# Three reorderings in a streaming encoder layer: where the sample sums and the keys' low part are split, which of two gate products comes first, and when the last hidden forms are made

## The chip, the cores and the metric

The kernel runs on one core of one Trainium2 chip. Its engines are named as in the profile: PE (matrix products), PEld (its weight loads), DVE (elementwise on vectors), ACT (activations, copies, casts), POOL (further elementwise work and a DMA queue), SP (a DMA queue). The metric is the time of one execution on the device in microseconds (us), median of the runs shown.

## The reference

One layer is computed for 512 prompt frames and 64 frames of a running stream, 576 in all, in fp32. Cut to what matters:

```python
hn = rmsnorm(x, g_norm1);  proj = hn @ w_in            # 2048 -> q, k, v (8 heads x 128), gb, gc, hc (1024 each)
z = q @ k.T / sqrt(128)                                # strictly causal
log_1mb = where(mask, log_sigmoid(-z), 0)
after = cumsum(log_1mb, axis=3, reverse=True) - log_1mb
w = where(mask, exp(log_sigmoid(z) + after), 0);  o_attn = w @ v
o_conv = gb * conv3_causal(gc * hc)
x = x + concat(rmsnorm(o_attn), rmsnorm(o_conv)) @ w_out
x = x + (silu(h2 @ w_gate) * (h2 @ w_up)) @ w_down     # h2 = rmsnorm(x, g_norm2), 2048 -> 5632 -> 2048
```

The running stream's 64 frames see 512 cached keys and values as well as their own.

## The kernel before

**Products in two parts.** Each fp32 operand is split into a high part (rounded to the product's format by an ACT cast) and a low part (DVE subtracts the high part from the source). A product of two operands is then three matmuls: high by high, low by high, high by low. `split(hi, lo, src)` issues the cast on ACT and the subtraction on DVE. Tiles that end in h and l (`qh`, `ql`, `kh`, `kl`, `sph`, `spl`, `ph1`, `pl1`) are such pairs; `whl` holds both parts of a weight block.

**Seven products instead of eight.** The large products run in units: two blocks of 128 output columns by two halves of 288 frames. A unit takes seven products, numbered `p_` = 1 to 7, of 24 matmuls each (fewer in the down projection). `run(n, p_)` issues product p_ of unit n; `prepare(n, p_)` splits the weight block that it needs, four places ahead in a list `order` (`AHEAD` = 4). Sums of weight blocks are made on DVE by `weight_sums` (lines L344 to L352). Products 1, 6, 5 and, later, 3 add up in one PSUM bank `psy`; after 1, 6 and 5 ACT copies what stands there (`part`, L427). Products 7 and 4 add up in a second bank, `psw`, and product 2 has a third, `psx`. After product 5 DVE adds a part and the bank to make results (L1491): for units 0 and 1 first half (0, 1) from bank `psv`, then half (1, 1) from `psw`. Units 0 and 1 of the feed-forward stage are "early": their product 3 has its own bank `psv`, taken from the three banks of the pool that `psy` comes from.

**What sets the order.** PE's instructions stand in the order in which the code issues them. The Python code advances generators by ticks: one tick is three matmuls of a large product, and a generator yields the number of ticks until its next step. In the attention and the gate/up stages a scheduler orders ACT, DVE, POOL and SP by its own estimate; `tc.issue_after(x)` holds work back behind instruction x. From the last gate/up units on, the order of these engines is the code's own (`manual_schedule`).

**Attention.** Eight heads pass through `attend(h)`, a new one every 29 ticks, between matmuls of the output projection (`pjo`). A head computes scores by key blocks 2, 1, 0 into banks z2, z1, z0, their softplus, sums over later keys by triangular products, and then, block by block, a mask (DVE, L1214), an exponential (ACT, L1216) and a split of the weights (`weights(b)`). For block 2 there are two masks, since block 3 shares its bank. The stream's own sums lie in `sp`, split into `sph` and `spl` and used by `sample_weights` (L1204 to L1207). The next head's queries and keys are split from `qf` and `kf` into `qh`, `ql`, `kh`, `kl`; PE first reads them for the next head's block 2 (L1161).

**Last hidden forms.** Gate and up columns come in 22 pairs. For each pair DVE makes seven combinations ("forms"), split and stored to `hid_dram`, which the down projection reads. Those of the last pair are made by `last_forms`, a generator that starts with a wait of 34 ticks and runs beside the first down products.

Of the kernel before, what the change touches and what calls it, by code (L numbers as in the profile page):

```python
# [10 lines left out]
F32 = mybir.dt.float32  # L11
F32R = mybir.dt.float32r
AF = mybir.ActivationFunctionType
ALU = mybir.AluOpType
PSUM = bass.MemoryType.PSUM

P = 128
TP = 512
# [6 lines left out]
NH = 8  # L25
# [76 lines left out]
def tile_hybrid_stream_step(  # L102
# [6 lines left out]
    nc = tc.nc  # L109
# [116 lines left out]
    def split(hi, lo, src, lo_eng=None):  # L226
        cast = nc.scalar.copy(out=hi, in_=src)  # L227
        (lo_eng or nc.vector).tensor_tensor(out=lo, in0=src, in1=hi.bitcast(F32), op=ALU.subtract)  # L228
        return cast.ins
# [731 lines left out]
    for E, h, lag in ((e1[0], 2, 8), (e1[1], 3, 22), (e0[0], 0, 36), (e0[1], 1, 50)):  # L961
# [4 lines left out]
    opening = [(0, 1), (0, 2), (1, 1), (0, 3), (0, 6), (1, 2), (0, 5), (0, 7), (1, 3), (0, 4), (1, 6), (2, 1), (1, 5),  # L966
               (1, 7), (2, 2), (1, 4), (2, 6), (2, 7), (2, 5)]
    order = [(n - NA, p_) for n, p_ in opening]
# [35 lines left out]
    qf, kf = (bpool.tile([P, T], F32, name=name) for name in ("qf", "kf"))  # L1004
    qh, ql, kh, kl = (bpool.tile([P, TP], F32R, name=name) for name in ("qh", "ql", "kh", "kl"))
# [4 lines left out]
    m01, mneg = (bpool.tile([P, P], F32, name=name) for name in ("m01", "mneg"))  # L1010
# [3 lines left out]
    sph, spl = (bpool.tile([P, T], F32R, name=name) for name in ("sph", "spl"))  # L1014
# [5 lines left out]
    def load_qk(h):  # L1020
        nc.sync.dma_start(out=qf, in_=qk_dram[h, 0])
        nc.sync.dma_start(out=kf, in_=qk_dram[h, 1])

    def split_qk():
        split(qh, ql, qf[:, :TP])
        split(kh, kl, kf[:, :TP])
# [7 lines left out]

    load_qk(0)
    split_qk()
    load_cached_keys(0)
    fetch_v(0)
# [111 lines left out]
    def attend(h):  # L1150
        pr, ph, pl, s1h, s1l, sp = (bt[n] for n in ("pr", "ph", "pl", "s1h", "s1l", "sp"))
        pb = [pr[0], pr[1], pr[2][:, :256], pr[2][:, 256:]]
        z, zb = {}, {}

        def scores(i):
            kk, q0 = slice(i * P, (i + 1) * P), i * P
# [39 lines left out]
        for b in (2, 1, 0):  # L1196
            nc.gpsimd.tensor_tensor(out=sums[:, b * TS : (b + 1) * TS], in0=sums[:, (b + 1) * TS : (b + 2) * TS],
                                    in1=sp[:, (b + 1) * TS : (b + 2) * TS], op=ALU.add)
# [12 lines left out]

        def weights(b):
            for i in ((2, 3) if b == 2 else (b,)):
                nc.vector.scalar_tensor_tensor(out=zb[i][:, :P], in0=zb[i][:, :P], scalar=0.0, in1=mneg,  # L1214
                                               op0=ALU.min, op1=ALU.add)
            nc.scalar.activation(out=pr[b][:, : full[b]], in_=z[b][:, : full[b]], func=AF.Exp)  # L1216
            return split(ph[b], pl[b], pr[b][:, : width[b]])

# [6 lines left out]
        mm(zb[2], trir, ph[2], stop=False, **kw)  # L1225
        mm(zb[2], trir, pl[2], stop=True, **kw)
        behind = weights(2)
        if h + 1 < NH:
            with tc.issue_after(behind):
                split_qk()  # L1230
        yield 4
        mm(zb[1], trir, ph[1], stop=False, **kw)
        mm(zb[1], trir, pl[1], stop=False, **kw)
        mm(zb[1][:, P:], neg1r, s1h, stop=False, **kw)
        mm(zb[1][:, P:], neg1r, s1l, stop=True, **kw)
        behind = weights(1)
        with tc.issue_after(behind):
            split(sph, spl, sp)
        yield 4
        mm(zb[0], trir, ph[0], stop=False, **kw)  # L1240
        mm(zb[0], trir, pl[0], stop=False, **kw)
        mm(zb[0][:, P:], neg1r, s0h, stop=False, **kw)
        mm(zb[0][:, P:], neg1r, s0l, stop=True, **kw)
        weights(0)
        hi, lo = mixa[h]
        ga, accA = col("ga", h), bt["accA"]
# [45 lines left out]
    def heads():  # L1292
        yield 9
        open_b()
        yield 3
        for h in range(NH):
            pipe.spawn(attend(h))
            yield PERIOD
# [135 lines left out]
    def put_form(fp, n, src):  # L1434

        t = tmp.tile([P, 2, HALF], F32R, tag="hl", name="form")
        split(t[:, 0], t[:, 1], src)
        q = nc.gpsimd if fp == NFP - 1 else nc.sync
        q.dma_start(out=hid_dram[fp][2 * n - 2 : 2 * n].rearrange("f p t -> p f t"), in_=t.bitcast(F32))  # L1439
# [26 lines left out]
    def last_forms(s10):  # L1466
        fp, h, tt = NFP - 1, hid.pop(NFP - 1), nc.vector.tensor_tensor
        s00, s01, s11 = h[0, 0], h[0, 1], h[1, 1]
        yield 34
        tt(out=s01, in0=s01, in1=gates.pop((0, 1)), op=ALU.mult)  # L1470
        yield 5
        tt(out=s10, in0=s10, in1=R2[:, :HALF], op=ALU.mult)
        tt(out=s10, in0=s10, in1=gates.pop((1, 0)), op=ALU.mult)
        for n, out, a, b in ((2, s10, None, None), (5, s00, s01, s00), (7, s01, s01, s11), (6, s11, s11, s00),
                             (4, s10, s10, s11)):
            yield 10
            if a is not None:
                tt(out=out, in0=a, in1=b, op=ALU.subtract)
            put_form(fp, n, out)

    def finish(kind, fp, c, i, ps, part=None):

        a, b = HALVES[i]
        if kind == "gate":
            s = gates[c, i] = tmp.tile([P, HALF], F32, tag="r" if i else "y", name="gs")
        else:
            s = tmp.tile([P, HALF], F32, tag="sq", name="ut") if c == i else h2pool.tile([P, HALF], F32, tag="hx", name="ux", bufs=2)
        if part is None:
            nc.vector.tensor_tensor(out=s, in0=ps, in1=R2[:, a:b], op=ALU.mult)
        else:  # L1490
            nc.vector.tensor_tensor(out=s, in0=ps, in1=part, op=ALU.add)  # L1491
            if kind == "up" and fp == NFP - 1 and (c, i) == (1, 0):
                pipe.spawn(last_forms(s))
                return
            nc.vector.tensor_tensor(out=s, in0=s, in1=R2[:, a:b], op=ALU.mult)
        if kind == "up" and fp == NFP - 1 and (c, i) == (0, 1):
            hid[fp][c, i] = s
            return
        if kind == "gate":
            nc.scalar.activation(out=s, in_=s, func=AF.Silu)  # L1500
            return
        nc.vector.tensor_tensor(out=s, in0=s, in1=gates.pop((c, i)), op=ALU.mult)
        hid.setdefault(fp, {})[c, i] = s
        put_forms(fp, c, i)

    slots = {}

    order = [(0, 1), (0, 2), (1, 1), (0, 3), (0, 6), (1, 2), (0, 7), (0, 5)] + opening[8:]
    early = {0, 1}
    for n in range(2, NU):  # L1510
        if n == NGU - 2:
# [183 lines left out]
```

## Time and profile before

| | us |
|---|---|
| median of 3 runs | 2346.3 (2346.07 to 2347.65) |
| profiled execution, its own time | 2347.48 |
| span of that execution, first to last instruction | 2345.8 |
| PE busy | 2332.0 (99% of the span) |
| DVE busy | 1940.0 (83%) |
| ACT busy | 1239.2 (53%) |
| POOL busy | 294.2 (13%) |

The mean granted clock of PE is 1.000. The attention stage lies between about 587 and 757 us of the span, the first gate and up products begin at 858.67 us, and the last forms fall between 1854 and 1880 us. Times in rows of the timeline are microseconds from the start of the span: start, duration, engine, line, operation, output<-inputs, shapes and count; in brackets stands how long the engine had been idle before the row and what ended the idle time.

### The profile page before, as it was taken

How to read it: one execution, taken by the hardware profiler on the slowest of the kernel's cores; microseconds unless marked ns; L12 is line 12 of the kernel's file. 1: busy time of each engine (PE TensorE's matmuls, PEld its weight loads, DVE VectorE, ACT ScalarE, POOL GpSimd, SP SyncE). 2: the span in 40 equal slices, each digit the busy share in tenths (PEclk: the TensorE clock that was granted, in tenths of full speed). 3: DMA queues.
4: the chain of work that ended last, by engine and by line, in shares of the span. 5: the costliest groups of instructions: out<-in, count | busy, mean ns of one | idle time of the engine just before them, and what ended most of it. 6: DMA issues, size and time to landing. Idle time of an engine off the chain costs nothing. (4 is left out here: it accounts for less than half of the span.)

```text
span 2345.8 us, 43802 instructions
## 1 busy us (share of the span) xinstructions
PE 2332.0 (99%) x17561; PEld 2321.6 (99%) x17561; DVE 1940.0 (83%) x2834; ACT 1239.2 (53%) x2244; POOL 294.2 (13%) x374
## 2 busy tenths in 40 slices
PE   9999999999999999999999999999999999999999
PEld 8999999999999999999999999999999999999998
DVE  8889889797777898888888888888888778887875
ACT  8556656455887564444444444444444444444454
POOL 0211121120332320000000000000000002431211
PEclk9999999999999999999999999999999999999999
DMA  8444243436753454444444444444444937875642
GB/s 270 137 122 123 90 142 103 149 116 208 202 143 109 168 198 126 154 141 136 154 128 149 148 134 149 138 139 153 127 150 140 356 112 229 231 218 187 201 130 82
DMA packets 482867, 368.85 MB, mean 157 GB/s; under 512 B 11630, under 2 KB 465064, under 8 KB 482664
## 3 DMA queue, kind: packets, MB, share of 16 engines
q1 hardware_dynamic: 475848, 356.58, 47.5%
q0 software_dynamic: 6384, 9.21, 2.3%
q8 instruction: 137, 2.24, 0.4%
q14 instruction: 66, 0.54, 0.1%
q10 hardware_dynamic: 432, 0.27, 0.0%
HBM read 285.52 MB, written 80.49 MB: 156 GB/s over the span
## 5 line engine op out<-in xcount | busy, mean ns | idle before, releaser
L228 DVE TENSOR_TENSOR whl<-raw_a,whl 128x1024 fp32r<-128x1024 f32 (+4 forms) x384 | 435.8, 1135 | 61.2 <-ACT whl L227 59.9
L404 PE MATMUL psy<-t,whl 128*128 128x288 f32 x3000 | 449.8, 295 | 0.0
L227 ACT CAST whl<-raw_a 128x1024 fp32r<-128x1024 f32 (+4 forms) x384 | 360.0, 939 | 137.7 <-PE psx L404 46.4
L404 PE MATMUL psy<-h_s,whl 128*128 128x288 f32 x2766 | 417.4, 295 | 0.6 <-ACT part L427 0.6
L404 PEld LDWEIGHTS psy<-t,whl 128*128 128x128 f32 x3000 | 414.8, 188 | 0.2
L404 PE MATMUL psw<-t,whl 128*128 128x288 f32 x2688 | 390.3, 295 | 0.0
L404 PEld LDWEIGHTS psy<-h_s,whl 128*128 128x128 f32 x2766 | 383.7, 188 | 1.2 <-ACT part L427 1.1
L404 PEld LDWEIGHTS psw<-t,whl 128*128 128x128 f32 x2688 | 367.0, 188 | 0.2
L228 DVE TENSOR_TENSOR whl<-raw_b,whl 128x1024 fp32r<-128x1024 f32 (+5 forms) x234 | 253.3, 1083 | 88.0 <-ACT whl L227 87.1
L227 ACT CAST whl<-raw_b 128x1024 fp32r<-128x1024 f32 (+5 forms) x234 | 211.0, 904 | 211.0 <-issue 75.2
L427 ACT COPY part<-psy 128x288 f32<-128x288 f32 x309 | 122.8, 397 | 345.0 <-PE psy L404 343.8
L404 PE MATMUL psx<-h_s,whl 128*128 128x288 f32 x1164 | 170.9, 295 | 0.0
L227 ACT CAST whl<-s 128x1024 fp32r<-128x1024 f32 (+5 forms) x103 | 95.2, 925 | 122.8 <-PE psw L404 115.0
L404 PEld LDWEIGHTS psx<-h_s,whl 128*128 128x128 f32 x1164 | 159.8, 188 | 0.0
L404 PE MATMUL psy<-t12a,whl 128*128 128x288 f32 x1056 | 150.9, 296 | 0.0
L404 PE MATMUL psw<-t34a,whl 128*128 128x288 f32 x1056 | 150.6, 295 | 0.0
L404 PEld LDWEIGHTS psy<-t12a,whl 128*128 128x128 f32 x1056 | 143.5, 188 | 0.3
L404 PEld LDWEIGHTS psw<-t34a,whl 128*128 128x128 f32 x1056 | 143.7, 188 | 0.0
L228 DVE TENSOR_TENSOR whl<-s,whl 128x1024 fp32r<-128x1024 f32 (+5 forms) x103 | 109.8, 1066 | 20.2 <-ACT whl L227 19.5
L1439 POOL DMA_DIRECT2D hid_dram<-form x7 | 5.2, 738 | 954.1 <-DVE form L228 945.8
L223 PE MATMUL pjo<-mixc,whi 128*128 128x288 f32 x512 | 119.0, 300 | 0.0
L223 PE MATMUL pjo<-mixa,whi 128*128 128x288 f32 x512 | 102.8, 296 | 0.0
(591 smaller groups left out, 3953.3 us busy)
## 6 DMA issues: line engine op xcount, KB each, us to landing
hid_dram<-form SPq DMA_DIRECT2D x147, 288.0 KB, 2.8
raw_a<-in_w_in_dram SPq DMA_DIRECT2D x22, 1024.0 KB, 5.5
raw_b<-in_w_in_dram SPq DMA_DIRECT2D x22, 1024.0 KB, 6.1
raw_b<-in_w_gate_dram SPq DMA_DIRECT2D x22, 1024.0 KB, 7.8
raw_b<-in_w_up_dram SPq DMA_DIRECT2D x22, 1024.0 KB, 6.5
raw_a<-in_w_gate_dram SPq DMA_DIRECT2D x22, 1024.0 KB, 5.8
raw_a<-in_w_up_dram SPq DMA_DIRECT2D x22, 1024.0 KB, 5.5
h_s<-hid_dram SPq DMA_DIRECT2D x10, 2016.0 KB, 11.0
```

What stands on the lines that cost most here:

```text
L223: mm(ps, w_[:, k, csl], x_[:, a:b], start=(k == 0 and n == 0), stop=(k == nk - 1 and n == 2))
L227: cast = nc.scalar.copy(out=hi, in_=src)
L228: (lo_eng or nc.vector).tensor_tensor(out=lo, in0=src, in1=hi.bitcast(F32), op=ALU.subtract)
L404: mm(ps, whl[:, w_, j, :], x_, start=(start and j == 0 and q == 0), stop=(j == len(xs_) - 1 and q == 2), skip_group_check=True)
L427: nc.scalar.copy(out=t, in_=st["y"])
L1439: q.dma_start(out=hid_dram[fp][2 * n - 2 : 2 * n].rearrange("f p t -> p f t"), in_=t.bitcast(F32))
```

## The change

Three places are edited. No operation is added or left out.

1. In `attend`, the split of the stream's sums (`sph`, `spl`), which stood behind block 1's exponential, is issued behind the cast of block 2's weights, ahead of the next head's split. The next head's queries are split there as before and its keys cast there; the keys' low part `kl` is issued by itself, held back behind the mask of block 1.
2. At the start of the gate/up stage, product 4 of unit 0 is run ahead of product 3 of unit 1 (before: behind it).
3. `last_forms` waits 36 ticks instead of 34 before its first step.

```diff
+    def low(hi, lo, src):
+        nc.vector.tensor_tensor(out=lo, in0=src, in1=hi.bitcast(F32), op=ALU.subtract)
...
-        z, zb = {}, {}
+        z, zb, masked = {}, {}, []
...
-                nc.vector.scalar_tensor_tensor(out=zb[i][:, :P], in0=zb[i][:, :P], scalar=0.0, in1=mneg,
-                                               op0=ALU.min, op1=ALU.add)
+                m = nc.vector.scalar_tensor_tensor(out=zb[i][:, :P], in0=zb[i][:, :P], scalar=0.0, in1=mneg,
+                                                   op0=ALU.min, op1=ALU.add)
+            masked.append(m.ins)
...
         behind = weights(2)
-        if h + 1 < NH:
-            with tc.issue_after(behind):
-                split_qk()
+        with tc.issue_after(behind):
+            split(sph, spl, sp)
+            if h + 1 < NH:
+                split(qh, ql, qf[:, :TP])
+                nc.scalar.copy(out=kh, in_=kf[:, :TP])
...
-        behind = weights(1)
-        with tc.issue_after(behind):
-            split(sph, spl, sp)
+        weights(1)
+        if h + 1 < NH:
+            with tc.issue_after(masked[-1]):
+                low(kh, kl, kf[:, :TP])
...
-        yield 34
+        yield 36
...
-    order = [(0, 1), (0, 2), (1, 1), (0, 3), (0, 6), (1, 2), (0, 7), (0, 5)] + opening[8:]
+    order = [(0, 1), (0, 2), (1, 1), (0, 3), (0, 6), (1, 2), (0, 7), (0, 5), (0, 4), (1, 3)] + opening[10:]
```

`opening[8]` and `opening[9]` are (1, 3) and (0, 4), so the second list swaps these two and is the same from the eleventh entry on.

The first place is DVE in the third head (`h` = 2), where the next head's parts are made. `hbe` is the low part of block 2's weights, z1 and z0 are the banks being masked, `x2` is the output projection's result. Before:

```order
L228 TENSOR_TENSOR hbe_6843<-pr2_6746,hbe_6843 128x256
L228 TENSOR_TENSOR ql_6729<-qf_6726,qh_6728 128x512
L228 TENSOR_TENSOR kl_6731<-kf_6727,kh_6730 128x512
L1214 SCALAR_TENSOR_TENSOR z1_7352<-z1_7352,mneg_6738 128x128
L1089 TENSOR_TENSOR x2_3_6961<-pjo_7479,accc_1925 128x288
L1214 SCALAR_TENSOR_TENSOR z0_7385<-z0_7385,mneg_6738 128x128
L228 TENSOR_TENSOR pl1_6750<-hbl_6840,ph1_6749 128x384
L228 TENSOR_TENSOR spl_6744<-hbl_6841,sph_6743 128x576
```

and now, with the same names:

```order
L228 TENSOR_TENSOR hbe_6843<-pr2_6746,hbe_6843 128x256
L1217 SCALAR_TENSOR_TENSOR z1_7352<-z1_7352,mneg_6738 128x128
L228 TENSOR_TENSOR spl_6744<-hbl_6841,sph_6743 128x576
L228 TENSOR_TENSOR ql_6729<-qf_6726,qh_6728 128x512
L1025 TENSOR_TENSOR kl_6731<-kf_6727,kh_6730 128x512
L228 TENSOR_TENSOR pl1_6750<-hbl_6840,ph1_6749 128x384
L1092 TENSOR_TENSOR x2_3_6961<-pjo_7479,accc_1925 128x288
L1217 SCALAR_TENSOR_TENSOR z0_7385<-z0_7385,mneg_6738 128x128
```

`spl` and the mask of z1 have moved from behind `kl` to ahead of it; `pl1` has moved ahead of the mask of z0.

The second place is DVE at the start of the gate/up stage, from the sums of unit 1's weights to the two gate results that follow product 5 of unit 0 (`gs_10422` from `psv`, `gs_10426` from `psw`, the bank that product 4 adds to). `whl_10363` is the block of product (0, 4) before and `whl_10322` the same block now; `whl_10327` and `whl_10364` are that of (1, 3); `whl_10392` is that of (1, 6). Before:

```order
L348 TENSOR_TENSOR raw_b_8814<-raw_b_8814,raw_a_100 128x8x128
L350 TENSOR_TENSOR raw_a_100<-s1_10322,raw_a_100 128x8x128
L352 TENSOR_TENSOR raw_a_100<-raw_a_100 128x8x128
L1491 TENSOR_TENSOR ut_10355<-psx2_10330,part_10263 128x288
L228 TENSOR_TENSOR whl_10363<-raw_b_8814,whl_10363 128x1024
L228 TENSOR_TENSOR whl_10327<-raw_a_100,whl_10327 128x1024
L1495 TENSOR_TENSOR ut_10355<-ut_10355,R2_10116 128x288
L1502 TENSOR_TENSOR ut_10355<-ut_10355,gs_10256 128x288
L228 TENSOR_TENSOR whl_10392<-raw_a_100,whl_10392 128x1024
L228 TENSOR_TENSOR form_10359<-ut_10355,form_10359 128x288
L1491 TENSOR_TENSOR gs_10422<-psv_10268,part_10420 128x288
L1491 TENSOR_TENSOR gs_10426<-psw_10367,part_10420 128x288
```

and now:

```order
L348 TENSOR_TENSOR raw_b_8814<-raw_b_8814,raw_a_100 128x8x128
L228 TENSOR_TENSOR whl_10322<-raw_b_8814,whl_10322 128x1024
L350 TENSOR_TENSOR raw_a_100<-s1_10359,raw_a_100 128x8x128
L1498 TENSOR_TENSOR ut_10351<-psx2_10326,part_10263 128x288
L352 TENSOR_TENSOR raw_a_100<-raw_a_100 128x8x128
L1502 TENSOR_TENSOR ut_10351<-ut_10351,R2_10116 128x288
L1509 TENSOR_TENSOR ut_10351<-ut_10351,gs_10256 128x288
L228 TENSOR_TENSOR whl_10364<-raw_a_100,whl_10364 128x1024
L228 TENSOR_TENSOR form_10355<-ut_10351,form_10355 128x288
L228 TENSOR_TENSOR whl_10392<-raw_a_100,whl_10392 128x1024
L1498 TENSOR_TENSOR gs_10422<-psv_10268,part_10420 128x288
L1498 TENSOR_TENSOR gs_10426<-psw_10367,part_10420 128x288
```

The same twelve instructions stand ahead of the end of `gs_10426` in both; three splits of weight blocks and the sums have changed places among themselves.

The third place is ACT beside the last forms. `form_20843` and `form_20849` are the same form, as are `form_20890` and `form_20896`; `part` are the copies of the bank that PE adds to next. Before:

```order
L227 CAST whl_20834<-raw_a_100 128x768
L227 CAST form_20843<-ut_20308 128x288
L427 COPY part_20859<-psy_20759 128x288
L227 CAST whl_20861<-raw_b_8814 128x640
L227 CAST whl_20881<-raw_b_8814 128x640
L227 CAST form_20890<-ux_20514 128x288
L427 COPY part_20906<-psy_20759 128x288
L227 CAST whl_20909<-raw_a_100 128x768
L227 CAST form_20932<-ut_20445 128x288
L427 COPY part_20936<-psy_20912 128x288
```

and now:

```order
L227 CAST whl_20834<-raw_a_100 128x768
L227 CAST form_20849<-ut_20308 128x288
L427 COPY part_20859<-psy_20757 128x288
L227 CAST whl_20861<-raw_b_8814 128x640
L227 CAST whl_20881<-raw_b_8814 128x640
L227 CAST form_20896<-ux_20514 128x288
L427 COPY part_20906<-psy_20757 128x288
L227 CAST whl_20909<-raw_a_100 128x768
L427 COPY part_20931<-psy_20912 128x288
L227 CAST whl_20933<-raw_a_100 128x768
L227 CAST form_20944<-ut_20445 128x288
```

The first two pairs of form and copy stand as they did; the third form has moved behind its copy and one more cast.

## The prediction

> **What bounds the kernel now.** I read the page's busy times first, then the list of what PE waited for, then the timeline around each wait that the change touches.
>
> ```profile
> PE 2332.0 (99%) x17561; PEld 2321.6 (99%) x17561; DVE 1940.0 (83%) x2834; ACT 1239.2 (53%) x2244; POOL 294.2 (13%) x374
> ```
>
> PE is busy in 2332.0 of the span's 2345.8 us. No matmul is added or dropped, so the change can only move PE's waits. Here they are, over the whole span, without the wait for the first input (engine, line waited for: us in total, times, longest):
>
> ```profile
> PE psv L404 <- ACT part L427: 1.3, 1, 1.3
> PE zs L1205 <- DVE spl L228: 1.0, 3, 0.4
> PE psy L404 <- ACT part L427: 0.6, 2, 0.4
> PE zs L1204 <- ACT sph L227: 0.3, 1, 0.3
> ```
>
> Each edit sits at one of them: the split of the sums at the waits for `spl` and `sph`, the swap at the wait of `psv`, the later forms beside the two waits of `psy`. So at most a few us can be gained, and the question is what is late next at each place.
>
> **The swap of (0, 4) and (1, 3).** PE, then ACT, then DVE, at that place:
>
> ```profile
> 881.93 2.93 PE L404 MATMUL psy<-t,whl 128*128 128x288 f32 x21
> 884.70 0.56 PE L404 MATMUL psy<-t12z,whl 128*128 128x288 f32 x3
> 886.52 0.67 PE L404 MATMUL psv<-h_z,whl 128*128 128x288 f32 x3 [1.27 <-ACT part L427]
> 889.83 3.33 PE L404 MATMUL psw<-t,whl 128*128 128x288 f32 x24
> ...
> 885.74 0.43 ACT L227 CAST form<-ut 128x288 fp32r<-128x288 f32 x1 [1.49 <-DVE ut L1502]
> 886.08 0.39 ACT L427 COPY part<-psy 128x288 f32<-128x288 f32 x1
> ...
> 887.13 0.45 DVE L1491 TENSOR_TENSOR gs<-psv,part 128x288 f32<-128x288 f32 x1
> 887.50 0.44 DVE L1491 TENSOR_TENSOR gs<-psw,part 128x288 f32<-128x288 f32 x1
> ```
>
> A matmul starts every 0.132 us here (21 from 881.93 to 884.70), so (1, 3) could have started at 884.70 + 3 x 0.132 = 885.10. It started at 886.52: lost 1.42 us, of which the list shows 1.27. It needed a bank that the copy `part` frees, at 886.47. That loss goes, since (0, 4) now stands between.
>
> But (0, 4) adds to `psw`, and DVE must first have read from `psw` the result of (0, 7): the second `gs`, done at 887.50 + 0.44 = 887.94. Before, (1, 3) covered this: (0, 4) started at 889.83 and waited for nothing. Now (0, 4) wants to start at 885.10. How early can that `gs` come? DVE is full there:
>
> ```profile
> 877.00:888.00 11.00, 9.73 (x74) 9.50 (x73) 10.83 (x15) 4.96 (x7) 0.00 (x0) 1.00 0.52 175
> ```
>
> The third busy column, DVE, has 10.83 of 11.00 us. The new order puts the same instructions ahead of `gs`, so without new gaps it ends at 887.94 again and PE starts 0.05 later (as 886.52 after 886.47), at 887.99: lost 2.89, against 1.42. One gap is new: the split for (1, 3) now follows soon upon the sum L352 that it reads, and ACT's cast lies between.
>
> ```profile
> 880.99 1.23 DVE L352 TENSOR_TENSOR raw_a<-raw_a 128x1024 f32<-128x1024 f32 x1
> 882.25 2.00 ACT L227 CAST whl<-raw_a 128x1024 fp32r<-128x1024 f32 x2 [2.25 <-DVE raw_a L352]
> 884.77 0.45 DVE L1495 TENSOR_TENSOR ut<-ut,R 128x288 f32<-128x288 f32 x1
> 885.25 0.46 DVE L1502 TENSOR_TENSOR ut<-ut,gs 128x288 f32<-128x288 f32 x1
> ```
>
> The cast starts with the sum's end and takes about 1.0 (2.00 for two); meanwhile DVE has the two `ut`, 0.48 + 0.46 = 0.94. With hand-overs I take a gap of 0.2. The sum: 2.89 + 0.2 - 1.42 = +1.7 us. Bounds: +1.4 (no gap) to +2.4 (a cast late by its whole length, 1.0). What follows is later by that much and has more slack for it; the operands of both products are ready long before (the casts at 882.25 include one for (1, 3)).
>
> On waits of this length the Trainium skill, TensorE: Matmul & The Clock Gate, section "Part 1: The HAM clock gate", has a rule against this change: after an idle window of about 3.4 us, free-running, the array goes back to half its clock until it has been busy for such a window. By it a wait of 2.9 us costs nothing more and a longer one may; it is a rival below, priced from rows.
>
> **The sums ahead of the keys.** The low part `spl` was late; now it stands ahead of `ql` and `kl`, which PE needs sooner. What goes first, by the rows that write or read `spl`:
>
> ```profile
> L228 DVE TENSOR_TENSOR spl<-hbl,sph x8: 746/752/759, 605.5 to 751.1; 128x576 fp32r<-128x576 f32 x8
> ...
>   PEld zs L1205: 2.0, 4
> ```
>
> The waits for `spl` and `sph` are 1.0 + 0.3 = 1.3 us in PE's list; the weight loads waited 2.0 for `spl` alone. In the third head PE's own starts show the ratio:
>
> ```profile
> 647.68 0.29 PE L223 MATMUL pjo<-mixc,whi 128*128 128x288 f32 x1
> 648.25 0.42 PE L1204 MATMUL zs<-sph,trir 128*128 128x320 f32 x1 [0.29 <-ACT sph L227]
> 649.05 0.42 PE L1205 MATMUL zs<-spl,trir 128*128 128x320 f32 x1 [0.38 <-DVE spl L228]
> ```
>
> From 647.68 to 649.05 it would be 0.13 + 0.14 without waits; it is 1.37, so 1.10 is lost where the list has 0.67. 1.3 x 1.10 / 0.67 = 2.1 us: my value, between 1.3 (the list itself) and 2.7 (twice it).
>
> `spl` now takes about the turn on DVE that `ql` had (645.06 in the rows below), 3 us ahead of 648.23, so all of this goes.
>
> What comes: `kl` is pushed back by one `spl`, 0.75 less the overlap of neighbours on DVE, 0.08 (`ql` below is 0.69 long and `kl` starts 0.60 behind its start): 0.67. Its room, per head, is from its end to PE's second score product of the next head:
>
> ```profile
> 625.21 0.68 DVE L228 TENSOR_TENSOR kl<-kf,kh 128x512 fp32r<-128x512 f32 x1
> 626.17 0.28 PE L1161 MATMUL z<-qh,kl 128*128 128x256 f32 x1
> ...
> 645.06 0.69 DVE L228 TENSOR_TENSOR ql<-qf,qh 128x512 fp32r<-128x512 f32 x1
> 645.66 0.68 DVE L228 TENSOR_TENSOR kl<-kf,kh 128x512 fp32r<-128x512 f32 x1
> 646.27 0.29 DVE L1214 SCALAR_TENSOR_TENSOR z<-z,mneg 128x128 f32<-128x128 f32 x1
> 646.55 0.28 PE L1161 MATMUL z<-qh,kl 128*128 128x256 f32 x1
> ...
> 603.80 0.68 DVE L228 TENSOR_TENSOR kl<-kf,kh 128x512 fp32r<-128x512 f32 x1
> 605.78 0.27 PE L1161 MATMUL z<-qh,kl 128*128 128x256 f32 x1
> ```
>
> Second head: 626.17 - 625.89 = 0.28 of room, so about 0.4 is lost. Third: 0.20 of room, and the mask of z1 (0.29 less the overlap, 0.2) now stands ahead too: up to 0.7, less what PE already lost one head before; 0.8 to 1.3 for the two with the refill of a stopped stream, I take 1.1. The first head has 604.48 to 605.78, 1.30, and nothing is lost. The heads behind the third have room like that, but only because PE had been held up by `spl` in the third, fourth, fifth and last; with these waits gone PE arrives sooner and meets the keys, or in the last head the next late tile. I charge 0.6 for all of them (0 to 0.9). Sum: -2.1 + 1.1 + 0.6 = -0.4 us, between -1.6 and +0.9.
>
> SP's queue passes only one swap of two loads here (`cV` ahead of `vtok` once) and POOL's order shifts by one add; neither is waited for at a place in PE's list, so nothing. ACT has the same casts in another order, `sph` ahead of `qh` and `kh`: 0.57, inside the 0.67 of `spl`.
>
> **The last forms.** Both waits of `psy` come from a copy that stands behind the cast of a form:
>
> ```profile
> 1862.52 0.83 ACT L227 CAST whl<-raw_a 128x768 fp32r<-128x768 f32 x1 [1.46 <-DMA raw_a<-in_w_down_dram]
> 1865.62 0.43 ACT L227 CAST form<-ut 128x288 fp32r<-128x288 f32 x1 [2.26 <-DVE ut L1478]
> 1865.96 0.39 ACT L427 COPY part<-psy 128x288 f32<-128x288 f32 x1
> 1866.40 1.06 PE L404 MATMUL psy<-h_s,whl 128*128 128x288 f32 x6 [0.21 <-ACT part L427]
> 1871.49 1.06 PE L404 MATMUL psy<-h_s,whl 128*128 128x288 f32 x6 [0.42 <-ACT part L427]
> ```
>
> The form waits for DVE, DVE's turn for the weights that landed at 1862.5. These two pairs keep their places in the new order, so both waits stay. The forms that do move were not waited for; the last store, from POOL's queue, leaves two ticks later (six matmuls, 0.8 us), and its reader comes much later. 0, between -0.6 (both waits go) and +0.4 (one more such wait).
>
> **The sum.** +1.7 - 0.4 + 0 = +1.3 us. The profiled execution took 2347.48, span 2345.8 and 1.7 around it, and stands 1.2 above the median of 2346.3; against itself the sum gives 2348.8. For the median I add it to the median: 2347.6. 0.2% of the time is 4.7 us, about what a measurement of this kernel can tell from no change.
>
> **The rivals.**
> *The change does what it seems meant for.* Both waits end and nothing takes their place: -1.4 - 2.1 gives 2342.8. For it: the 1.30 of room in the first head. Against it: DVE's 10.83 of 11.00, which would have to be 2.9 us emptier. Half of it, the keys on time (none of the 1.1 and 0.6) beside the new wait of (0, 4), gives 2345.9 and lies inside my range. 10% for the whole.
> *The keys are late in every head.* If each of seven heads loses the whole 0.67, 4.7 replaces my 1.7: 2350.6. For it: all heads run the same order. Against it: 1.30 of room in the first. It decides where room is under 0.67 in most heads. 12%.
> *The clock falls.* If the wait of (0, 4) grows to 3.9 us (the gap at its bound of 1.0), it comes near the one idle time behind which the array runs at half rate, 4.01 us at the start of the kernel. The rows there show the price:
>
> ```profile
> 4.01 1.09 PE L555 MATMUL psx<-ident,xin 128*128 128x128 f32 x4 [4.01 <-DMA xin<-in_x_prompt_dram]
> 8.27 0.44 PE L690 MATMUL pj<-b12a,whi 128*128 128x288 f32 x1
> 8.51 0.44 PE L690 MATMUL pj<-b,whi 128*128 128x288 f32 x1
> ...
> 9.99 1.07 PE L555 MATMUL psx<-ident,xin 128*128 128x128 f32 x8
> ```
>
> There matmuls start 0.24 apart, not 0.132, from 4.01 until about 9.9; in the last row eight of a shape take what four took in the first. These 5.9 us would take 5.9 x 0.132 / 0.24 = 3.2 at full rate, 2.7 lost. With a gap of 1.0 for 0.2 it is +1.3 + 0.8 + 2.7 = +4.8, slower than before by over 0.2%: 2351.1. No wait in the middle of before is that long, and the gap must be at its bound: 5%. By the rule of the Trainium skill named above a whole free-running window must be idle, which a wait of just over 3.4 us seldom holds.
>
> **How the numbers follow.** Forecast 73%, the rivals 10, 12 and 5. The range takes the terms' bounds (-1.6 + 1.4 - 0.6 = -0.8; +0.9 + 2.4 + 0.4 = +3.7) and the spread of three runs (0.2 below, 1.4 above the median): 2345.3 below and 2351.4 above if all fell together. I widen the lower end to 2344.5, towards the first rival, which it still leaves out, and end at 2350.8, which holds the second and leaves out the clock. Faster by over 0.2% needs more than all three listed waits: 3%. Slower by over 0.2%: the clock's upper end and part of the late keys, 7%. Same 90%.
>
> **What would show it.** Right: PE's list loses `psv` and gains a wait of `psw` on DVE `gs` of about 2.7 us near 888; `spl` and `sph` leave it, `kl` enters it in two to four heads; the two of `psy` stay at 1866 and 1871. Wrong: a `psw` wait under 1.4, `kl` absent, or a granted clock under 1 behind 888.

## The result and the profile after

The changed kernel took 2350.48 us in the median of 22 runs (2347.8 to 2352.55), the kernel before 2346.44 in the median of 22 (2345.36 to 2348.24). The ratio is 1.0016, with a 95% interval of 1.0011 to 1.0022: 4.0 us slower. The profiled execution of the changed kernel took 2348.91 with a span of 2347.2, only 1.4 above the span of before. So two things want an answer: where the profile's 1.4 us come from, and why the medians stand 4.0 apart.

What PE waited for in the changed kernel, over the whole span (us in total, times, longest):

```profile
PE psw L404 <- DVE gs L1498: 2.2, 1, 2.2
PE z L1164 <- DVE kl L1025: 1.3, 3, 0.6
PE psy L404 <- ACT part L427: 0.8, 2, 0.5
```

The waits for `psv`, `spl` and `sph` are gone, and `psw` and `kl` have come. The waits of the last forms have stayed.

The timeline of PE, then ACT, then DVE, at the swap in the changed kernel (start, duration; in brackets the idle time ahead and what ended it):

```profile
884.88 0.56 PE L404 MATMUL psy<-t12z,whl 128*128 128x288 f32 x3
887.64 3.40 PE L404 MATMUL psw<-t,whl 128*128 128x288 f32 x24 [2.19 <-DVE gs L1498]
...
894.05 2.94 PE L404 MATMUL psy<-t,whl 128*128 128x288 f32 x21
...
885.48 0.40 ACT L427 COPY part<-psy 128x288 f32<-128x288 f32 x1 [0.20 <-PE psy L404]
...
885.54 1.22 DVE L228 TENSOR_TENSOR whl<-raw_a,whl 128x1024 fp32r<-128x1024 f32 x1
886.68 0.45 DVE L1498 TENSOR_TENSOR gs<-psv,part 128x288 f32<-128x288 f32 x1
887.04 0.45 DVE L1498 TENSOR_TENSOR gs<-psw,part 128x288 f32<-128x288 f32 x1
```

(0, 4) waits for the second `gs`, as forecast. The part that both read was ready at 885.88; DVE came to it only at 886.68, behind the 1.22 us split of a weight block.

How far apart the same two points of the program lie tells what an edit costs, whatever happened earlier. For the swap I take the last three matmuls of (0, 5) and the first of (1, 6); between them stand 51 matmuls, 6.7 us at 0.132. In the changed kernel it is 894.05 - 884.88 = 9.17. In before it is 893.01 - 884.70 = 8.31, with this row:

```profile
893.01 2.94 PE L404 MATMUL psy<-t,whl 128*128 128x288 f32 x21
```

For the attention I take the first head's `po<-hbe` and the first matmul of the gate stage, in before and then in the changed kernel:

```profile
604.83 0.60 PE L1268 MATMUL po<-hbe,vz 128*128 128x256 f32 x3
```

```profile
604.15 0.60 PE L1275 MATMUL po<-hbe,vz 128*128 128x256 f32 x3
858.86 2.31 PE L404 MATMUL psy<-h_s,whl 128*128 128x288 f32 x16
```

With 858.67 for before (the start of the first gate and up products, given above) it is 253.84 before and 254.71 after: +0.87. One execution is enough here: the other traces that are read below give 253.85 to 253.96 wherever attention is that of before, and 254.68 to 254.74 wherever it has the edit.

The `kl` tile of the changed kernel has the list of who waited for it:

```profile
  PEld z L1164: 2.9, 6
  PE z L1164: 1.3, 3
```

Six of seven heads wait for the keys. The sixth is the worst; DVE, then PE there:

```profile
708.09 0.29 DVE L1217 SCALAR_TENSOR_TENSOR z<-z,mneg 128x128 f32<-128x128 f32 x1
708.32 0.76 DVE L228 TENSOR_TENSOR spl<-hbl,sph 128x576 fp32r<-128x576 f32 x1
709.00 0.69 DVE L228 TENSOR_TENSOR ql<-qf,qh 128x512 fp32r<-128x512 f32 x1
709.60 0.69 DVE L1025 TENSOR_TENSOR kl<-kf,kh 128x512 fp32r<-128x512 f32 x1
...
709.39 0.38 PE L1164 MATMUL z<-qh,kh 128*128 128x256 f32 x1
710.34 0.38 PE L1164 MATMUL z<-qh,kl 128*128 128x256 f32 x1 [0.57 <-DVE kl L1025]
```

The two products start 0.95 apart, where 0.12 would do (256 columns, at 0.132 for 288): 0.83 lost behind a `kl` that stands behind `spl`.

### The profile page after: what moved, and what is told of

Read it like the earlier page. It is cut to its first block, busy times and chain, and to the rows that moved or that the text cites. A ratio compares the mean times of both kernels' runs of the same rounds, so it can differ in the third digit from the quotient of the medians.

```text
span 2347.2 us, 43803 instructions
## 1 busy us (share of the span) xinstructions
PE 2332.1 (99%) x17561; PEld 2321.7 (99%) x17561; DVE 1939.5 (83%) x2834; ACT 1238.9 (53%) x2244; POOL 297.6 (13%) x374
```

## The experiments

My theory after the result: the attention edit loses because the keys' low part is late in nearly every head, the swap because DVE is late with `gs`; the forms cost nothing. The rivals: one edit alone carries the whole loss. Then a second theory came out of the first four runs, that of the clock.

### Each edit alone

The attention edit (`a_alone`) is the attention part of the diff, without the swap and the later forms.

> The attention edit alone. Theory (late keys, of varying size): in the profile of the changed kernel the keys' low part was waited for in six of seven heads, 0.2 to 0.8 us each, some 3.7 us of lost starts against 2.4 before, yet its attention stage came out level with before and its median stood 4.0 us above. So this edit alone is slower by 1 to 3 us in the median, with a spread of single runs as wide as the changed kernel's (about 5 us), and PE's list shows kl in three or more heads and no spl. Rival 1 (the product swap carries the loss): within 0.5 us of before, spread like before's 3 us. Rival 2 (the parts add up from the swap and the forms): the same, within 0.5 us.

Measured: 2347.87 (2346.27 to 2348.63, 11 runs) against 2346.58 (33 runs), ratio 1.0004 (0.9995 to 1.0013): +1.3 us, with an interval that holds 0. The single runs spread over 2.4 us, not the 5 expected. Its trace agrees with the changed kernel's in the attention: 857.43 - 602.75 = 254.68, +0.84.

```profile
602.75 0.60 PE L1275 MATMUL po<-hbe,vz 128*128 128x256 f32 x3
857.43 2.97 PE L404 MATMUL psy<-h_s,whl 128*128 128x288 f32 x21
...
883.46 0.56 PE L404 MATMUL psy<-t12z,whl 128*128 128x288 f32 x3
884.63 0.66 PE L404 MATMUL psv<-h_z,whl 128*128 128x288 f32 x3 [0.61 <-ACT part L427]
...
891.08 2.94 PE L404 MATMUL psy<-t,whl 128*128 128x288 f32 x21
```

There is a second thing in these rows: the products stand in the order of before, yet the wait for `psv` is 0.61, not 1.27, and the stretch 891.08 - 883.46 = 7.62, not 8.31.

The forms alone (`c_alone`):

```
-        yield 34
+        yield 36
```

> The last forms two ticks later, alone. Theory: the two waits of psy at 1866 and 1872 stay, 0.2 to 0.7 us of lost starts each; a third, near 1999, was in the changed kernel's trace (0.3) and belongs to chance; the time is within 0.5 us of before. Rival (the later forms carry part of the loss): +0.7 us or more, and the wait near 1999 is there again.

Measured: 2347.04 (2344.96 to 2349.91, 11 runs), ratio 1.0001 (0.9992 to 1.0010). The waits of `psy` are 0.7 in sum where before had 0.6, and the wait of `psv` is again 0.6:

```profile
PE psy L404 <- ACT part L427: 0.7, 2, 0.5
PE psv L404 <- ACT part L427: 0.6, 1, 0.6
```

The wait near 1999 was not in its list. The forms cost nothing that these runs could tell. Its single runs spread over 5.0 us, with neither the swap nor the attention edit: eleven runs can scatter that far without either, and the spread, on which some of my expectations rest, proves little by itself.

The swap alone (`b_alone`) is the last line of the diff.

> The swap of (0, 4) and (1, 3) alone. Theory: psv's wait leaves the list and one wait of psw on gs of about 2.2 us stands near 888; lost starts there 2.4 against 1.4, so +1.0 us (0.7 to 1.5), spread of runs like before's. Rival 1 (the swap carries the whole loss of the changed kernel): +3 us or more, with the wide spread. Rival 2 (as in the theory of the late keys, but the swap gains by what follows): 0 or below.

Measured: 2349.24 (2347.58 to 2351.81, 11 runs), ratio 1.0013 (1.0005 to 1.0022): +2.7 us, more than double what I expected from the wait, with a wide spread (4.2 us). The trace shows why. PE's rows, and then busy times by stretch, of which the column behind the five engines is the granted clock:

```profile
884.50 0.56 PE L404 MATMUL psy<-t12z,whl 128*128 128x288 f32 x3
887.44 4.94 PE L404 MATMUL psw<-t,whl 128*128 128x288 f32 x24 [2.38 <-DVE gs L1491]
...
895.39 2.94 PE L404 MATMUL psy<-t,whl 128*128 128x288 f32 x21
```

```profile
886.00:888.00 2.00, 0.56 (x4) 0.59 (x5) 2.00 (x6) 0.74 (x2) 0.00 (x0) 1.00 0.50 171
888.00:890.00 2.00, 2.00 (x13) 2.00 (x12) 1.17 (x2) 0.51 (x2) 0.00 (x0) 0.69 1.06 317
890.00:892.00 2.00, 2.00 (x11) 2.00 (x10) 0.00 (x0) 0.00 (x0) 0.00 (x0) 0.50 0.61 181
892.00:894.00 2.00, 2.00 (x16) 2.00 (x16) 1.36 (x3) 1.40 (x2) 0.00 (x0) 0.95 0.04 12
```

Behind the stall of 2.38 us the clock fell to half. The same 24 matmuls took 4.94 us where they took 3.40 in the changed kernel's trace: 1.5 us on top of the wait. The stretch is 895.39 - 884.50 = 10.89.

### The clock, tested

First, the stall filled (`b_fill`): the swap, and 16 matmuls into a spare bank ahead of (0, 4). They are work that the result does not use.

```
+        if (n, p_) == (0, 4):
+            fill = misc("fill")[:, :HALF]
+            xh, xl = h2a[0]
+            for q in range(16):
+                mm(fill, operand[0, 4][:, 0, 0, :], xh, start=(q == 0), stop=(q == 15), skip_group_check=True)
         run(n, p_, n in early)
```

> The swap alone, with 16 matmuls of 288 columns ahead of (0, 4), into a bank that nobody reads; they add nothing to the result and take 16 x 0.132 = 2.1 us of the 2.5 that PE loses there. Theory (the clock: the stall lets the granted clock fall to half behind it, in part of the executions): the wait for gs stays, so (0, 4) starts no earlier, but no window behind it shows a clock under 1; the median is 1 to 1.5 us below the swap alone, the spread of single runs (4.2 us there) is that of before (about 2.6). Rival (only the wait counts, and the spread comes from elsewhere): median and spread as in the swap alone.

Measured: 2348.72 (2346.94 to 2349.68, 11 runs), ratio 1.0009 (1.0000 to 1.0017): 0.5 below the swap alone, less than I expected and too little for these intervals to tell apart. The spread is 2.7 us, that of before. The clock is 1.00 in every stretch there:

```profile
884.56 2.27 PE L1634 MATMUL fill<-h_s,whl 128*128 128x288 f32 x16
886.84 3.48 PE L404 MATMUL psw<-t,whl 128*128 128x288 f32 x24
```

```profile
888.00:890.00 2.00, 2.00 (x17) 2.00 (x16) 0.65 (x1) 0.00 (x0) 0.00 (x0) 1.00 1.12 337
```

Second, the stall shortened (`b_w_first`): in unit 0 DVE reads `psw` before `psv`.

```
-            if early:
+            if early and n != 0:
                 done(0, 1, st["v"], st["u4"])
             if "w" in st:
                 ...
                 done(1, 1, st["w"], st["u4"])
+            if early and n == 0:
+                done(0, 1, st["v"], st["u4"])
```

> The swap alone, with DVE reading psw ahead of psv in unit 0, so that the result for which (0, 4) waits comes one instruction (0.37 us) sooner. Theory of the clock: the stall falls from 2.5 to about 2.1 us, which saves 0.4, and the clock falls less often, which saves up to 1.5 more: 0.4 to 1.6 us below the swap alone. Rival (only the wait counts): 0.4 below, spread as there.

Measured: 2348.17 (2346.87 to 2350.97, 11 runs), ratio 1.0008 (0.9999 to 1.0017), 1.1 below the swap alone, with intervals that overlap. Its trace, too, has the fall, behind a shorter stall (PE's row, then the stretch with the clock):

```profile
886.07 4.98 PE L404 MATMUL psw<-t,whl 128*128 128x288 f32 x24 [2.15 <-DVE gs L1493]
```

```profile
888.00:890.00 2.00, 2.00 (x11) 2.00 (x10) 0.25 (x1) 0.00 (x0) 0.00 (x0) 0.50 1.14 342
```

Third, the changed kernel traced three times more (`after_again`, `after_third`, `after_fourth`).

> The changed kernel once more, for a second trace. Theory of the clock: the wait of psw near 888 is again 2.0 to 2.6 us; where the time is over 2350 the windows behind 888 show a granted clock under 1, where it is below 2349.5 they don't. Rival: the time differs by waits in other places, with the clock at 1.

> The changed kernel, third trace. Theory: its two traces so far show no fall of the clock and times of 2348.9 and 2348.5, below its median of 2350.5; so with a time over 2350 a stretch of about 14 matmuls 0.240 us apart follows the stall at 887, without it the time is under 2349.7. Rival: a time over 2350 with the clock at 1 behind 887.

> The changed kernel, fourth trace, as for the third: over 2350 with a stretch at half clock behind the stall at 887, or under 2349.7 without one; the rival is a time over 2350 with the clock at 1 there.

Measured: 2348.49, 2348.70 and 2349.87. The waits of `psw`, the three in this order, and a stretch of the last by the clock:

```profile
887.29 3.40 PE L404 MATMUL psw<-t,whl 128*128 128x288 f32 x24 [2.28 <-DVE gs L1498]
```

```profile
887.40 1.03 PE L404 MATMUL psw<-t,whl 128*128 128x288 f32 x6 [2.30 <-DVE gs L1498]
```

```profile
887.57 0.90 PE L404 MATMUL psw<-t,whl 128*128 128x288 f32 x5 [2.51 <-DVE gs L1498]
```

```profile
888.00:890.00 2.00, 2.00 (x17) 2.00 (x16) 1.30 (x2) 0.64 (x2) 0.00 (x0) 1.00 1.06 305
```

None has the fall, and none took over 2350. But 2349.87 is more than the 2349.7 expected of an execution without a fall: that trace has four waits for `psy`, 2.2 us in sum, where the other three have 0.5 to 0.8. So some of the spread comes from other waits, as the rival said, and the changed kernel was not caught in the fall, not even behind the longest stall of all, 2.51.

Fourth, the changed kernel with the same filler (`after_fill`).

> The changed kernel with the same 16 matmuls ahead of (0, 4), which add nothing to the result. Theory (in part of its executions the changed kernel loses some 1.5 us to the half clock behind the stall): the stall stays in length, the clock stays at 1, and the median falls 0.7 to 1.5 us below the changed kernel's (4.0 above before: so 2.5 to 3.3 above), with single runs spread over 3 us where it had 4.8. Rival (the rest of the changed kernel's loss lies in attention): the median stays 4 us above before.

Measured: 2349.30 (2348.32 to 2350.63, 11 runs) against 2346.69, ratio 1.0011 (1.0002 to 1.0021): +2.6 us, spread 2.3. That is what the theory said, though the interval also holds the rival's +4.0.

**Where the stall lies.** The kept traces show what sets the two groups apart. Each holds the times at which the granted clock changed: up once, between 8.96 and 11.70 us, and down for good behind the last matmul. Between the two lie 2334.72 us in nine of the fourteen traces, 2331.30 in four and 2338.13 in one: 684, 683 and 685 times 3.413. The falls in the middle lie on the same grid; in `b_alone` the clock goes down at 888.78, 257 such steps behind its rise at 11.55, and up one step later, at 892.19. So the clock changes only at the ends of steps of 3.41 us, and where these begin differs from execution to execution. PE's idle time can then be counted step by step, as the step's length less PE's busy time. Four of them, in `b_w_first`, `b_alone`, `after_again` and `after_fourth` (length, then PE's busy time):

```profile
883.40:886.81 3.41, 1.26 (x9) 1.02 (x9) 3.41 (x7) 2.03 (x4) 0.00 (x0) 1.00 0.35 117
885.37:888.78 3.41, 1.34 (x10) 1.37 (x11) 3.41 (x7) 1.88 (x4) 0.00 (x0) 1.00 0.50 163
883.47:886.88 3.41, 1.54 (x12) 1.30 (x10) 3.20 (x5) 2.80 (x5) 0.00 (x0) 1.00 0.51 166
886.19:889.61 3.42, 2.04 (x15) 2.07 (x16) 3.11 (x6) 1.08 (x3) 0.00 (x0) 1.00 0.76 230
```

| trace | wait ahead of (0, 4), us | most idle time in one step, us | clock in the next step |
|---|---|---|---|
| `b_w_first` | 2.15 | 2.15 | 0.50 |
| `b_alone` | 2.38 | 2.07 | 0.50 |
| `after_again` | 2.28 | 1.87 | 1.00 |
| `after_third` | 2.30 | 1.79 | 1.00 |
| `after_fourth` | 2.51 | 1.38 | 1.00 |
| changed kernel, first trace | 2.19 | 1.23 | 1.00 |

The longest wait was cut in two by the end of a step, and the shortest lay within one. Over all steps of the fourteen traces, those behind the last matmul with them, every step with 2.07 us or more of idle PE was followed by a fall and none with less than 1.84; of two between, the 1.84 was and the 1.87 was not.

The mean clock on record for the other executions says a little more. A fall in the middle costs half of 3.41, 1.7 us or 0.0007 of the time, so an execution with a mean of 1.000 cannot have had one. In `b_alone` the four with 1.000 are the four fastest (2347.58 to 2348.99), and the slowest, 2351.81, has 0.998. Of the changed kernel's 22, three have 1.000, all below 2350. But `after_fill` has 2350.63 with 1.000, so a time over 2350 is no proof of a fall, and 0.999 decides nothing, since the clock also falls behind the last matmul.

### The other ways out

The sums' split directly behind the keys (`sums_behind_keys`), not ahead of them:

```
             with tc.issue_after(behind):
                 split_qk()
+        with tc.issue_after(behind):
+            split(sph, spl, sp)
...
-        behind = weights(1)
-        with tc.issue_after(behind):
-            split(sph, spl, sp)
+        weights(1)
```

> Before, with the sums' split issued directly behind the next head's keys, behind block 2's weights (no wait of the keys is put behind a mask). Theory (the loss in attention is the keys' turn on DVE, not the sums' early place): spl and sph leave PE's list as in the changed kernel, kl stays on time in most heads, and the time falls by 1 to 2.4 us against before. Rival (DVE is full there, so whatever goes ahead makes the next tile late): another tile, pl or the masks, enters the list in three or more heads and the time is within 0.7 us of before or above it.

Measured: 2346.45 (11 runs) against 2346.58, ratio 0.9998 (0.9989 to 1.0007). In the trace the attention is 856.82 - 603.58 = 253.24, 0.60 below before. Neither sums nor keys are in PE's list (the second fence); the weights of the blocks are:

```profile
603.58 0.60 PE L1268 MATMUL po<-hbe,vz 128*128 128x256 f32 x3
856.82 2.97 PE L404 MATMUL psy<-h_s,whl 128*128 128x288 f32 x21
```

```profile
PE po L1268 <- ACT ph L227: 0.7, 1, 0.7
PE po L1268 <- DVE pl L228: 0.2, 1, 0.2
```

Both theories were half right: the keys' turn was what cost the change its gain, and most of that gain went to the next late tile.

A bank of its own for product 3 of unit 1, together with the sums behind the keys (`psv_own_sums`, and once more as `own_sums_again`); the order of products is that of before:

```
-            st["v"] = ps_pj.tile([P, HALF], F32, tag="pj", name="psv")
+            st["v"] = misc("psv")[:, :HALF] if n == 1 else ps_pj.tile([P, HALF], F32, tag="pj", name="psv")
```

> Order of products as before; product 3 of unit 1 gets a bank of its own, and the sums' split stands directly behind the next head's keys. Theory: the wait of psv (0.7 to 1.4 us in four traces) leaves the list and nothing replaces it, since (0, 4) stays behind (1, 3); with the 0.6 us that the sums gain in attention by the trace, 1 to 2 us below before. Rival (DVE's late turn is what counts: the wait moves to (0, 4) for gs): within 0.5 us of before.

> Product 3 of unit 1 in a bank of its own and the sums behind the keys, once more, for a tighter interval: 1 to 2 us below before (it was 1.5 below, with an interval that held 0). If the gain was chance: within 0.5 us.

Measured: 2345.22 against 2346.72, ratio 0.9996 (0.9987 to 1.0005), and 2344.77 against 2346.69, ratio 0.9994 (0.9985 to 1.0003). Both medians lie below before, by 1.5 and 1.9, and neither interval alone excludes no change. In the trace the wait is gone and nothing has come in its place:

```profile
882.88 0.56 PE L404 MATMUL psy<-t12z,whl 128*128 128x288 f32 x3
883.28 0.56 PE L404 MATMUL psv<-h_z,whl 128*128 128x288 f32 x3
883.68 2.94 PE L404 MATMUL psv<-h_s,whl 128*128 128x288 f32 x21
886.46 3.33 PE L404 MATMUL psw<-t,whl 128*128 128x288 f32 x24
889.63 2.93 PE L404 MATMUL psy<-t,whl 128*128 128x288 f32 x21
```

From 882.88 to 889.63 it is 6.75, the 51 matmuls and nothing else. Here (0, 4) comes late enough for `gs`, which the swap took away.

## Why the prediction was right and where it was not

The outcome, 2350.48, lies in the range (2344.5 to 2350.8), near its upper end. The forecast's +1.3 was +4.0. That it lies inside is in part luck: the upper end was set to hold the rival of the late keys, whose price the runs do not show, and to leave out the falling clock, into which the swap alone did run.

- **The new wait of `psw`: right.** It came at 887.6 with 2.19 in the list (2.28 to 2.51 in the other traces; forecast about 2.7) and follows `gs` after `psv`'s, on a full DVE. It was shorter than forecast: `gs` ended at 887.49, 2.61 behind the start of the last three matmuls of (0, 5), where before it was 887.94 - 884.70 = 3.24.
- **What the swap saves: mis-sized, by one draw.** The 1.42 taken off was the loss in one execution. Where the order of before stands, three other traces have 0.61, 0.61 and 0.51 in place of 1.27. Against 7.62 of `a_alone` the changed kernel's 9.17 is +1.55; the four traces of each order average 9.31 and 7.77, +1.5. My +1.7 was near this by luck, because both its terms were too large.
- **The clock: the step that failed.** The rival "the clock falls" had 5%, on the condition that the wait grows to 3.9 us, because the only half-rate matmuls in the trace of before stand behind 4.01 us of idle time. The runs show it behind 2.38 and 2.15. Its price of 2.7 was too high: 1.5. By the rule of the Trainium skill, TensorE: Matmul & The Clock Gate, "Part 1: The HAM clock gate", that I weighed, the clock goes down after an idle window of about 3.4 us; these traces disagree, since no idle time here was that long. The section also calls the window free-running. Here the traces agree: the steps of 3.41 us begin elsewhere in each execution, and so 2.38 us fell in one and 2.51 passed in another. A step need not be wholly idle, as I had taken from the rule: 2.07 us of its 3.41 were enough.
- **The sums: right. The keys: mis-sized.** `spl` and `sph` left the list. The keys were charged 1.1 in two heads and 0.6 in all others, with nothing in the first. Weight loads and matmuls waited for `kl` in six heads. I had seen that the later heads' room was only there because PE had been held up, and still charged too little: the sixth alone lost 0.83. The -0.4 for the attention is +0.85 (254.71 and 254.68 against 253.84), near its upper bound of +0.9. (Its lower bound of -1.6 has the keys at 1.1; with their own lower bound of 0.8 it would be -1.9.) The rival of the late keys gave 2350.6, close to the outcome, and was right that nearly every head is late; but its 4.7 us is not there. If the sums saved their 2.1, the keys cost 2.1 + 0.85, some 3.0, between my 1.7 and the rival's 4.7, so that its number came out is chance.
- **The forms: right.** 0 was forecast; `c_alone` stands at 1.0001 (0.9992 to 1.0010).
- **The base.** Before's profiled execution was 1.0 above its median and the changed kernel's 1.6 below its own, so the two spans hide 2.6 of the 4.0.

The sum by the traces: 0.85 + 1.55 + 0 = 2.4, and about 3.9 where the clock falls. The four traces of the changed kernel average 2349.0 and its filled version has 2349.3, 2.3 to 2.6 above before, without a fall in any of these traces. The median of 2350.48 is 1.5 above that average, which is what the fall cost in `b_alone`. How often the changed kernel has it can only be estimated, from the steps: if they begin anywhere with equal chance, a stall of 2.3 us puts 2.07 us into one step in (3.41 + 2.3 - 2 x 2.07) / 3.41 = 0.46 of the executions, and 1.84 us in 0.60. About half, then; four traces without a fall are no rare draw (1 in 16), but the average would rise by only some 0.8 us. What is shown is that the swap's stall can bring the clock down, when it does so, what that costs, and that the two traces with the stall filled have no fall. Of the 4.0 us, 2.3 to 2.6 are shown in the changed kernel, some 0.8 is this estimate, and the rest stays open; the interval of the 4.0 is 2.6 to 5.2 us.

## What to carry to other kernels

A wait that is taken out of one place by reordering has its price where the reordered instruction needs something itself: look what the overtaken work covered (here the 3.2 us of (1, 3) covered `gs`), and free the resource instead where that can be done, as the spare bank did. Where one tile is moved ahead on a full engine, charge every tile behind it in every repetition, and take the room of the later repetitions as it is without the earlier stalls. And a stall of PE of over 2 us may cost 1.5 us more than its length, when most of it falls into one step of the clock; one trace of each kernel is not enough to see that, nor to size a wait of 1 us.

## What the hardware showed that I had not expected

The granted clock of PE fell to 0.50 behind idle times of 2.38 and 2.15 us in the middle of a kernel that is 99% busy, and 24 matmuls then took 4.94 and 4.98 us instead of 3.40. Idle times of 2.19, 2.28, 2.30 and 2.51 us at the same place passed without it. So the length of the idle time alone does not decide. What does, in all fourteen traces, is the idle time within one step of 3.41 us, the steps lying elsewhere in each execution: from 2.07 us on the clock fell for the next step, and below 1.84 it never did.
